# A two-layer decoder trunk: output and down projections with the tokens stationary and 512 weight columns moving

## The chip, the cores and the metric

The kernel runs on one core of one Trainium2 chip. The metric is the device time of one execution in microseconds (us); lower is better. The engines are named as the profile names them: PE is the tensor engine (PEld its weight loads), DVE the vector engine, ACT the scalar engine, POOL the general-purpose engine, and SP the engine whose queue issues the transfers.

## The reference

256 tokens of 2048 columns pass through two layers, all in float32. Cut to what matters here:

```python
for l in range(DEPTH):                                  # 2 layers
    h = rms_norm(x, norm_mix[l])                        # over 2048 columns
    proj = h @ w_in[l]                                  # 5446 columns, split among three kinds of heads
    o_a = diff_attention(dq, dk, dv, ...)               # 4 heads: (softmax(q1 k1) - lam softmax(q2 k2)) v, normed
    o_b = forgetting_attention(fq, fk, fv, ff, ...)     # 6 heads: logits + c[t] - c[s]
    o_c = latent_attention(mq, mkv, ...)                # 6 heads from low-rank q and kv
    x = x + concat(o_a, o_b, o_c) @ w_out[l]            # 2048 x 2048
    h = rms_norm(x, norm_ffn[l])
    x = x + square(relu(h @ w_ff_up[l])) @ w_ff_down[l] # 2048 x 8192 and 8192 x 2048
```

All attention is causal, over blocks of 128 queries, with normed queries and keys.

## The kernel before

**Arithmetic.** Weights and activations are multiplied as two float32r parts, hi and lo, that add up to the float32 value. `load_w` (L186) loads a raw weight tile of 128 x 1024 (five buffers), ACT copies it to `whi` (L193), DVE subtracts that to get `wlo` (L194), with three buffers of each. A product is hi x hi, lo x hi and hi x lo.

**Two forms of product.** `product_t` (L254) holds the weights stationary, 128 x 128 at a time. The moving operand is a chunk of the activations: both parts of 256 tokens, 512 columns, for `whi`, and the hi part alone, 256 columns, for `wlo`. So a weight tile of 1024 columns is 8 matmuls of 512 and 8 of 256, and the result has the weights' columns in the partitions and both parts of the tokens beside each other in one bank of PSUM. `product` (L269) holds 128 tokens stationary and lets the weights move, 512 columns wide in mq, dq, dk and dv: a tile of 1024 columns is two chunks by 512, and 12 matmuls of 512 columns. The input projection has the second form; the output projection (`wo`, L740 to 760), the up projection (`up_block`) and the down projection (`down_block`) have the first.

**The residual** `x` lies transposed: 16 chunks of 128 model columns in the partitions, by 256 tokens. `add_to_x` (L265) adds both halves of a bank to it, each 128 x 256, on DVE. `Norm.add` (L231) takes a finished chunk, multiplies it by the gain and splits it (`ht`), and squares it, summing the squares of all chunks on POOL; `Norm.scale` (L244) then sums over the partitions with eight one-column matmuls (`ss`) on PE. Layer 0's input comes transposed from memory (`FirstInput`, L364). The output is written transposed.

**Order.** A layer runs mq, mkv, the up projections of the latent heads, then fq, fk and fv in two halves, dq, dk, dv, the output projection, eight blocks of the feed-forward. Behind the products stand the steps of the attention heads, as generators in `Background` (`bg`, L80): after each weight tile `bg.step()` writes out 1.25 stages on the average, and `bg.finish()` all that are left. A scheduler then sorts the instructions of each engine by when it expects them to be ready, so that on PE a transpose or a score often stands in the middle of a tile's matmuls. The names that matter below are: `dt`, the transposes of the latent down projections `qd` and `kvd`; `qk`, transposes of queries and keys (`fqk`, `dqk`) or of the differential heads' outputs (`osb`); `s`, the scores; `p`, the exponentials, from `exps` (L312); `pt`, the transposes of p; `o`, p times the values. In `diff_maps` (L676) a head has two scores, p2 is scaled and taken from p1, and the result is transposed.

**The feed-forward.** `up_block` (L796) makes 1024 columns of the inner layer in eight banks of 128 columns; `squared` (L781) scales, clips and squares them and splits them into `g`. `down_block` (L810) adds 1024 rows of the down projection to all 16 chunks of x, one weight tile and one bank per chunk. While one block goes down, the next has already gone up.

Of the kernel before, what the change touches and what calls it, by code (L numbers as in the profile page):

```python
# [11 lines left out]
F32 = mybir.dt.float32  # L12
# [4 lines left out]
ALU = mybir.AluOpType  # L17
# [20 lines left out]
# Columns of w_in by group, in the order in which the groups are computed.  # L38
# [25 lines left out]
# Parameters along the free dimension, the same in every partition.  # L64
# [11 lines left out]
N_EARLY = 8  # L76
# [48 lines left out]
def trunk_kernel(ctx: ExitStack, tc: tile.TileContext, ins: dict, out: bass.AP):  # L125
# [15 lines left out]

    def mm(out, lhsT, rhs, start, stop):
        nc.tensor.matmul(out, lhsT, rhs, start=start, stop=stop)  # L143
# [15 lines left out]
    # The tensor engine's clock rises only with work: products of zeros until the first data are there.  # L159
# [9 lines left out]
    x = cp.tile([P, NK, SEQ], F32, name="x")  # transposed: chunks of the model's columns by tokens  # L169
# [8 lines left out]
    # Halves of these stay zero: one head's 64 rows beside the other's in a full contraction.  # L178
# [22 lines left out]
    def split_to(dst, src, gain):  # L201
        """dst [P, 2 parts, n] <- src [P, n] * gain [P, 1]"""
# [21 lines left out]
    class Norm:  # L224
        """The next norm's input, chunk by chunk: times gain and split into h, and squared into sums."""

        def __init__(self, gain, name):
            self.gain, self.name, self.h = gain, name, []
            self.squares = ap.tile([P, 2 * SEQ], F32, tag="squares", name=f"squares_{name}", bufs=1)

        def add(self, k):  # L231
            if k % 2 == 0:
                self.h.append(parts_tile("ht", "ht"))
            split_to(self.h[k // 2][:, k % 2], x[:, k, :], self.gain[:, k:k + 1])
            if k % 2 == 1:
                pair = x[:, k - 1:k + 1, :].rearrange("p c t -> p (c t)")
                if k == 1:
                    nc.scalar.activation(self.squares, pair, AF.Square)
                else:
                    sq = ap.tile([P, 512], F32, tag="sq", name="sq")  # L240
                    nc.scalar.activation(sq, pair, AF.Square)
                    nc.gpsimd.tensor_tensor(self.squares, self.squares, sq, ALU.add)

        def scale(self):  # L244
            """[P, NT] reciprocal root mean square of the tokens"""
# [66 lines left out]
    def exps(s):  # L312
        """exp(s - max) and the reciprocals of its sums; p holds the negated masked scores in between."""
# [15 lines left out]
    def transposed_p(p):  # L329
        """[keys, queries]: keys 0:128 by queries 0:256, then keys 128:256 by queries 128:256."""  # L330
# [7 lines left out]
    def weighted_values(pT, v, dst):  # L338
        """dst [P, 2 parts, tokens] <- (p @ v) transposed"""
# [5 lines left out]
    def heads_transposed(pairs):  # L345
        """Two [tokens, 128] blocks in both halves of the tokens, transposed into one bank."""
# [6 lines left out]
    def rotate(v, cos, sin, n, h):  # L353
        """v [P, n, 2, h] in place, by angles [P, h]"""
# [9 lines left out]
    class FirstInput:  # L364
        def __init__(self, norm):
            self.norm, self.n = norm, 0

        def __len__(self):
            return NK // 2

        def __getitem__(self, j):
            if j == self.n:
                self.n += 1
                nc.sync.dma_start(x[:, 2 * j:2 * j + 2, :], ins["xT"][:, 2 * j:2 * j + 2, :])
                self.norm.add(2 * j)
                self.norm.add(2 * j + 1)
                if j == 4:
                    nc.sync.dma_start(cst, ins["cst"])
            return self.norm.h[j]

    norm = Norm(pp[0][:, PP["mix"]], "mix0")
    h = FirstInput(norm)

    for l in range(DEPTH):
# [57 lines left out]
        # sums: [q rope, k rope | q nope, k nope] by tokens  # L442
# [35 lines left out]
        # small parameters of the layer  # L478
# [85 lines left out]
        def forget_gates():  # L564
# [8 lines left out]
            # log sigmoid(z) = min(z, 0) - log(1 + exp(-|z|)), log(1 + e) = 2 atanh(e / (2 + e))  # L573
# [14 lines left out]
            # Their running sums c, in rows by head (and -c six rows on), as three bfloat16 parts that add up  # L588
            # to them, 32 rows apart; with ones beside them a product over the rows gives c[t] - c[s].
# [146 lines left out]
        # some columns without the last heads, while those are worked on  # L736
# [195 lines left out]
```

## Time and profile before

| | us |
|---|---|
| median of three runs | 2173.51 |
| the three runs | 2173.34 to 2173.85 |
| span of the profiled execution | 2171.8 |
| PE busy | 2161.0 (100%), 12288 matmuls |
| DVE busy | 1494.2 (69%) |
| ACT busy | 1080.5 (50%) |
| POOL busy | 41.9 (2%) |

The profile shows one execution from its first to its last instruction; 1.7 us of the median lie outside that span. The granted clock of PE is full in every slice. Matmuls are pipelined: the shown duration of one reaches into the next, so the cost of a matmul in a row of them is read from start to start. The chain that ended last is followed back from the last instruction, at each step to what released it. In a row of the timeline, "x8" says how many instructions of one kind stand together, the second number is the time from the first one's start to the last one's end, and square brackets hold the idle time before it and what ended it.

### The profile page before, as it was taken

The numbers are of one execution on the slowest core, as the hardware profiler recorded it, in microseconds if no ns is written. First come the engines' busy times: TensorE is split into PE (matmuls) and PEld (weight loads), VectorE is DVE, ScalarE is ACT, GpSimd is POOL, SyncE is SP. The second block draws the span as 40 slices with busy tenths as digits, with TensorE's granted clock in tenths as the row PEclk, the third lists the DMA queues.
The fourth block names the chain that finished last, engine by engine and source line by source line (L and its number), as shares of the span: only waits on it lengthen the run. The fifth ranks groups of instructions, "written<-read, shape, count | busy, mean of one in ns | idle before, by whom it ended". The sixth has DMA issues, their size and how long they took to land.

```text
span 2171.8 us, 32348 instructions
## 1 busy us (share of the span) xinstructions
PE 2161.0 (100%) x12288; PEld 1917.7 (88%) x12288; DVE 1494.2 (69%) x2632; ACT 1080.5 (50%) x1587; POOL 41.9 (2%) x37
## 2 busy tenths in 40 slices
PE   9999999999999999999999999999999999999999
PEld 7999888888888888888899998888888888888888
DVE  7876687666666666666868667975666666566666
ACT  6655465544444444544566555645444444435442
POOL 2000001000000000000100000010000000000000
PEclk9999999999999999999999999999999999999999
DMA  7545455565556555555555464465556555555555
GB/s 237 172 140 179 155 160 190 182 192 186 189 187 191 188 187 191 186 191 186 189 161 170 139 182 151 151 204 186 192 185 192 186 190 189 188 191 186 192 184 155
DMA packets 116940, 393.81 MB, mean 181 GB/s; under 512 B 13232, under 2 KB 15408, under 8 KB 116784
## 3 DMA queue, kind: packets, MB, share of 16 engines
q1 hardware_dynamic: 116784, 391.74, 57.1%
q8 instruction: 97, 1.59, 0.3%
q14 instruction: 59, 0.48, 0.1%
HBM read 389.59 MB, written 2.10 MB: 180 GB/s over the span
## 4 chain that ended last, share of the span: by engine, by line
PE 94%; DVE 3%; ACT 1%; issue 1%; DMA 0%; SPq 0%; DVEq 0%
PE u L143 33%; PE dn L143 33%; PE wo L143 8%; PE fq L143 3%; PE fk L143 3%; PE fv L143 2%; PE dk L143 2%; PE dq L143 2%; PE mq L143 2%; PE s L143 2%; PE mkv L143 1%; PE qup L143 1%; DVE wlo L194 1%; PE o L143 1%; PE qk L299 1%
## 5 line engine op out<-in xcount | busy, mean ns | idle before, releaser
L193 ACT ACTIVATE whi<-wraw 128x1024 fp32r<-128x1024 f32 (+3 forms) x781 | 789.8, 1013 | 994.8 <-PE dn L143 389.7
L194 DVE TENSOR_TENSOR wlo<-wraw,whi 128x1024 fp32r<-128x1024 f32 (+3 forms) x781 | 910.2, 1166 | 410.2 <-ACT whi L193 401.2
L143 PE MATMUL u<-ht,whi 128*128 128x512 f32 x2048 | 513.1, 392 | 0.0
L143 PE MATMUL dn<-g,whi 128*128 128x512 f32 x2048 | 512.8, 392 | 0.0
L143 PEld LDWEIGHTS dn<-g,whi 128*128 128x128 f32 x2048 | 368.4, 189 | 65.8
L143 PEld LDWEIGHTS u<-ht,whi 128*128 128x128 f32 x2048 | 368.2, 189 | 65.9
L267 DVE TENSOR_TENSOR x<-dn,x 128x256 f32<-128x256 f32 x512 | 215.4, 422 | 205.9 <-PE dn L143 205.6
L143 PEld LDWEIGHTS u<-ht,wlo 128*128 128x128 f32 x2048 | 279.4, 190 | 20.0
L143 PEld LDWEIGHTS dn<-g,wlo 128*128 128x128 f32 x2048 | 279.4, 190 | 19.9
L143 PE MATMUL dn<-g,wlo 128*128 128x256 f32 x2048 | 285.6, 282 | 0.0
L143 PE MATMUL u<-ht,wlo 128*128 128x256 f32 x2048 | 285.6, 282 | 0.0
L143 PE MATMUL wo<-mix,whi 128*128 128x512 f32 x512 | 136.6, 400 | 0.0
L143 PEld LDWEIGHTS wo<-mix,whi 128*128 128x128 f32 x512 | 91.4, 189 | 15.3
L143 PEld LDWEIGHTS wo<-mix,wlo 128*128 128x128 f32 x512 | 72.0, 190 | 6.8 <-DVE wlo L194 0.6
L143 PE MATMUL wo<-mix,wlo 128*128 128x256 f32 x512 | 75.1, 283 | 0.0
L319 ACT ACTIVATE p<-p,nm 128x128 f32<-128x128 f32 x80 | 35.8, 449 | 40.3 <-DVE nm L318 40.2
L208 DVE SCALAR_TENSOR_TENSOR ht<-x,pp,ht 128x256 fp32r<-128x256 f32 x64 | 53.2, 847 | 3.0 <-ACT ht L207 2.8
L143 PE MATMUL fq<-whi,ht 128*128 128x384 f32 x256 | 53.7, 349 | 0.0
L787 DVE TENSOR_TENSOR relu<-u,relu 128x256 f32<-128x256 f32 x128 | 53.6, 419 | 0.0
L143 PE MATMUL fk<-whi,ht 128*128 128x384 f32 x256 | 51.7, 343 | 0.0
L143 PE MATMUL fv<-whi,ht 128*128 128x384 f32 x256 | 51.0, 340 | 0.0
L786 ACT COPY relu<-u 128x256 f32<-128x256 f32 x128 | 46.0, 359 | 0.0
(249 smaller groups left out, 1716.4 us busy)
## 6 DMA issues: line engine op xcount, KB each, us to landing
wraw<-in_w_up SPq DMA_DIRECT2D x256, 512.0 KB, 3.4
wraw<-in_w_down SPq DMA_DIRECT2D x256, 512.0 KB, 3.4
wraw<-in_w_out_c SPq DMA_DIRECT2D x32, 512.0 KB, 4.3
wraw<-in_w_fv SPq DMA_DIRECT2D x32, 384.0 KB, 3.2
wraw<-in_w_fq SPq DMA_DIRECT2D x32, 384.0 KB, 3.3
wraw<-in_w_fk SPq DMA_DIRECT2D x32, 384.0 KB, 3.1
wraw<-in_w_out_a SPq DMA_DIRECT2D x32, 384.0 KB, 3.1
wraw<-in_w_dq SPq DMA_DIRECT2D x16, 512.0 KB, 4.5
```

The lines of the kernel that those rows point to most:

```text
L143: nc.tensor.matmul(out, lhsT, rhs, start=start, stop=stop)
L193: nc.scalar.activation(hi[:, cols], raw[:, cols], AF.Copy)
L194: nc.vector.tensor_tensor(lo[:, cols], raw[:, cols], hi[:, cols], ALU.subtract)
L208: nc.vector.scalar_tensor_tensor(dst[:, 1, :], src, gain, dst[:, 0, :], ALU.mult, ALU.subtract)
L267: nc.vector.tensor_tensor(x[:, k, :], acc[:, i * SEQ:(i + 1) * SEQ], x[:, k, :], ALU.add)
L299: nc.tensor.transpose(dst, src, ident)
L319: nc.scalar.activation(p[:, cols], p[:, cols], AF.Exp, bias=nm[:, i:i + 1], scale=-1.0, accum_out=z[:, i:i + 1])
L786: nc.scalar.copy(r[:, cols], u[i][:, SEQ:])
L787: nc.vector.tensor_tensor(r[:, cols], u[i][:, :SEQ], r[:, cols], ALU.add)
```

## The change

Every matmul and transpose is now passed to `keep_in_program_order`: PE issues them in the order in which they are written, and the scheduler moves only the other engines' instructions.

The residual lies by tokens, two tiles of 128 tokens by 2048 columns. Output and down projections take the second form: `product_x` holds 128 tokens stationary, and each block of them meets two pieces of 512 weight columns in turn (one piece in the last 1024 columns of the output projection and of each layer's last down block). A tile is 12 matmuls of 512 columns. `add_to_x` adds a bank of 512 columns. The down projection is cut into two halves of 1024 columns, four banks each, with eight weight tiles after another into the same banks; up and down blocks take turns with the two pools of PSUM. The output projection does its first 1024 columns with the first 12 heads while the differential heads are worked on, then finishes the steps that are left, then adds the last four heads.

`Norm.columns` gets the transposed input of the next product from x: four transposes of 128 x 128 on PE into one bank (`xt`), whose halves are multiplied by the gain and split as before. The squares are summed along the rows by ACT as it squares; `Norm.scale` needs no matmul. Layer 0's first norm still reads the transposed input from memory (`FirstNorm`, with POOL and `ss` as before) into x's place, and x itself is loaded by four transfers of 512 KB during fq and fk of layer 0. The first up block works on four banks at once, first all over the first half of the columns. The output is written by tokens.

```diff
+    def in_order(ins):
+        tc.keep_in_program_order(ins)
+
     def mm(out, lhsT, rhs, start, stop):
-        nc.tensor.matmul(out, lhsT, rhs, start=start, stop=stop)
+        in_order(nc.tensor.matmul(out, lhsT, rhs, start=start, stop=stop))
...
-    x = cp.tile([P, NK, SEQ], F32, name="x")
+    x = cp.tile([P, NT, D_MODEL], F32, name="x")
...
+        def columns(self, c0, n):
+            for q in range(c0 // 512, (c0 + n) // 512):
+                for t in range(NT):
+                    junk = sp.tile([P, 512], F32, tag="junk", name="junk")
+                    nc.scalar.activation(junk, x[:, t, q * 512:(q + 1) * 512], AF.Square, accum_out=self.sums[:, t, q:q + 1])
+            for k in range(c0 // P, (c0 + n) // P, 2):
+                b = acc_tile("xt")
+                for i in range(2):
+                    for t in range(NT):
+                        transpose_block(b[:, i * SEQ + t * P:i * SEQ + (t + 1) * P], x[:, t, (k + i) * P:(k + i + 1) * P])
+                h = parts_tile("ht", "ht")
+                for i in range(2):
+                    split_to(h[:, i], b[:, i * SEQ:(i + 1) * SEQ], self.gain[:, k + i:k + i + 1])
+                self.h.append(h)
+                yield
...
-    def add_to_x(acc, k):
-        for i in (1, 0):
-            nc.vector.tensor_tensor(x[:, k, :], acc[:, i * SEQ:(i + 1) * SEQ], x[:, k, :], ALU.add)
+    def product_x(accs, chunk, hi, lo, off, start, stop):
+        c, j = chunk
+        for part, w in ((0, hi), (1, hi), (0, lo)):
+            for t in range(NT):
+                for b, acc in enumerate(accs[t]):
+                    mm(acc, c[:, j, part, t * P:(t + 1) * P], w[:, off + b * 512:off + (b + 1) * 512],
+                       start and w is hi and part == 0, stop and w is lo)
+
+    def add_to_x(accs, c0):
+        for t in range(NT):
+            for b, acc in enumerate(accs[t]):
+                cols = x[:, t, c0 + b * 512:c0 + (b + 1) * 512]
+                nc.vector.tensor_tensor(cols, acc, cols, ALU.add)
...
     def transpose_block(dst, src):
-        nc.tensor.transpose(dst, src, ident)
+        in_order(nc.tensor.transpose(dst, src, ident))
...
+                if l == 0:
+                    cols = slice((2 * s + a) * 512, (2 * s + a + 1) * 512)
+                    nc.sync.dma_start(x[:, :, cols], ins["x"][:, :, cols])
...
+        out_columns(left, w_left, 0, HALF, 0, N_EARLY, bg.step)
         bg.finish()
...
+        out_columns(left, w_left, 0, HALF, N_EARLY, 16)
+        add_to_x(left, 0)
+        bg.add(norm.columns(0, HALF))
+        for q in range(2):
+            c0 = HALF + q * 512
+            right = [[t_tile("wo")] for _ in range(NT)]
+            out_columns(right, lambda i: ins["w_out_b"][l, q, i], c0, 512, 0, 16, bg.step)
+            add_to_x(right, c0)
+            bg.add(norm.columns(c0, 512))
...
+            def block(bank, w, c0, width):
+                n, per = width // 512, 1024 // width
+                accs = [[bank("dn") for _ in range(n)] for _ in range(NT)]
+                for i in range(0, N_FC, per):
+                    hi, lo = load_w(w(i // per), 1024)
+                    for k in range(per):
+                        product_x(accs, chunks[i + k], hi, lo, k * width, i + k == 0, i + k == N_FC - 1)
+                    bg.step()
+                add_to_x(accs, c0)
```

Three places where PE's row differs. The first is in dq of layer 0, where the transposes of the forgetting heads' queries and keys (`fqk`) come in. Before:

```order
L143 MATMUL dq_2268<-whi,ht 128x512 x2
L143 MATMUL dq_2269<-whi,ht 128x512 x2
L143 MATMUL dq_2268<-whi,ht 128x512 x2
L143 MATMUL dq_2269<-whi,ht 128x512 x2
L299 MATMUL qk<-cst,fqk_1860 128x128
L143 MATMUL dq_2268<-wlo,ht 128x512
L299 MATMUL qk<-cst,fqk_1861 128x128
L299 MATMUL qk<-cst,fqk_1860 128x128
L299 MATMUL qk<-cst,fqk_1861 128x128
L143 MATMUL dq_2268<-wlo,ht 128x512
L143 MATMUL dq_2269<-wlo,ht 128x512 x2
```

The same place in PE's row after the change:

```order
L148 MATMUL dq_2272<-wlo,ht 128x512 x2
L148 MATMUL dq_2273<-wlo,ht 128x512 x2
L359 MATMUL qk<-cst,fqk_1862 128x128
L359 MATMUL qk<-cst,fqk_1863 128x128
L359 MATMUL qk<-cst,fqk_1862 128x128
L359 MATMUL qk<-cst,fqk_1863 128x128
L148 MATMUL dq_2272<-whi,ht 128x512 x2
L148 MATMUL dq_2273<-whi,ht 128x512 x2
L148 MATMUL dq_2272<-whi,ht 128x512 x2
L148 MATMUL dq_2273<-whi,ht 128x512 x2
```

The eight matmuls by `whi` of the next tile, which stood ahead of these transposes, now stand behind them.

The second place is in dv of layer 0, at the transposes of the differential heads' queries and keys (`dqk`; the two numbers are the two halves of the tokens). Before:

```order
L143 MATMUL dv_2719<-wlo,ht 128x512 x2
L299 MATMUL qk<-cst,dqk_2265 128x128 x2
L143 MATMUL dv_2718<-whi,ht 128x512 x2
L143 MATMUL dv_2719<-whi,ht 128x512 x2
L143 MATMUL dv_2718<-whi,ht 128x512 x2
L143 MATMUL dv_2719<-whi,ht 128x512
L299 MATMUL qk<-cst,dqk_2266 128x128
L299 MATMUL qk<-cst,dqk_2265 128x128
L299 MATMUL qk<-cst,dqk_2266 128x128 x2
L299 MATMUL qk<-cst,dqk_2265 128x128
L299 MATMUL qk<-cst,dqk_2266 128x128
L143 MATMUL dv_2719<-whi,ht 128x512
```

After:

```order
L148 MATMUL dv_2723<-wlo,ht 128x512 x2
L359 MATMUL qk<-cst,dqk_2269 128x128
L359 MATMUL qk<-cst,dqk_2270 128x128
L359 MATMUL qk<-cst,dqk_2269 128x128
L359 MATMUL qk<-cst,dqk_2270 128x128
L359 MATMUL qk<-cst,dqk_2269 128x128
L359 MATMUL qk<-cst,dqk_2270 128x128
L359 MATMUL qk<-cst,dqk_2269 128x128
L359 MATMUL qk<-cst,dqk_2270 128x128
L148 MATMUL dv_2722<-whi,ht 128x512 x2
```

The seven matmuls of the next tile that stood between the first half's transposes and the second half's now follow all eight.

The third place is in the output projection of layer 0, at the second score of a differential head (`half_106`) and the transposes of p. Before:

```order
L143 MATMUL s<-kT,half_106 128x128
L143 MATMUL s<-kT,half_106 128x256
L143 MATMUL wo<-mix_0_841,whi 128x512 x2
L143 MATMUL wo<-mix_1_842,whi 128x512
L299 MATMUL pt<-cst,p 128x128
L143 MATMUL wo<-mix_1_842,whi 128x512
L143 MATMUL wo<-mix_2_843,whi 128x512
L299 MATMUL pt<-cst,p 128x128 x2
L143 MATMUL wo<-mix_2_843,whi 128x512
L143 MATMUL wo<-mix_0_841,wlo 128x256 x2
L143 MATMUL wo<-mix_1_842,wlo 128x256 x2
L143 MATMUL wo<-mix_2_843,wlo 128x256 x2
```

After:

```order
L148 MATMUL s<-kT,half_102 128x128
L148 MATMUL s<-kT,half_102 128x256
L148 MATMUL wo<-whi,mix_0_841 128x512 x8
L148 MATMUL wo<-wlo,mix_0_841 128x512 x4
L148 MATMUL s<-kT,half_106 128x128
L148 MATMUL s<-kT,half_106 128x256
L359 MATMUL pt<-cst,p 128x128 x6
L359 MATMUL qk<-cst,dqk_2269 128x128
L359 MATMUL qk<-cst,dqk_2270 128x128
```

Before, the three transposes shown are those of the head whose scores came earlier, and those of this head's p follow another nine to eleven products later; now the transposes of both heads follow at once on the score.

## Rows read from the trace of the kernel before

**Rows 1.** The page: busy engines (us, share, instructions), the transfer queue, the last chain.
```profile
PE 2161.0 (100%) x12288; PEld 1917.7 (88%) x12288; DVE 1494.2 (69%) x2632; ACT 1080.5 (50%) x1587; POOL 41.9 (2%) x37
...
q1 hardware_dynamic: 116784, 391.74, 57.1%
...
PE 94%; DVE 3%; ACT 1%; issue 1%; DMA 0%; SPq 0%; DVEq 0%
```

**Rows 2.** The chain of waits (start us, us, what), one down block.
```profile
464.82 44.69 PE dn L143 x256
```

**Rows 3.** The timeline (start us, us, engine, line, operation), PE, an up tile.
```profile
906.00 2.00 PE L143 MATMUL u<-ht,whi 128*128 128x512 f32 x8
907.84 1.11 PE L143 MATMUL u<-ht,wlo 128*128 128x256 f32 x8
```

**Rows 4.** The timeline, PE, a tile of mq in layer 1 and the next.
```profile
1098.55 1.98 PE L143 MATMUL mq<-whi,ht 128*128 128x512 f32 x8
1100.36 1.07 PE L143 MATMUL mq<-wlo,ht 128*128 128x512 f32 x4
1101.27 1.98 PE L143 MATMUL mq<-whi,ht 128*128 128x512 f32 x8
```

**Rows 5.** The page's costliest groups (count, busy us, mean ns, idle), dn and wo.
```profile
L143 PE MATMUL dn<-g,whi 128*128 128x512 f32 x2048 | 512.8, 392 | 0.0
...
L143 PE MATMUL wo<-mix,whi 128*128 128x512 f32 x512 | 136.6, 400 | 0.0
```

**Rows 6.** Timeline, PE, transposes in mkv of layer 1; the group pt (ns min/median/max).
```profile
1118.23 0.87 PE L299 MATMUL dt<-cst,qd 128*128 128x128 f32 x6
1118.86 0.85 PE L143 MATMUL mkv<-wlo,ht 128*128 128x326 f32 x4
...
L299 PE MATMUL pt<-cst,p x96: 270/272/328, 98.3 to 1376.5; 128*128 128x128 f32 x96
```

**Rows 7.** The timeline, PE, the sums of squares in layer 0's feed-forward.
```profile
379.43 1.05 PE L143 MATMUL ss<-cst,squares_ffn 128*128 128x1 f32 x8
380.34 2.09 PE L143 MATMUL u<-ht,whi 128*128 128x512 f32 x8
```

**Rows 8.** Groups by line (ns min/median/max), DVE, adds of 256 and scalings of 512 columns.
```profile
L267 DVE TENSOR_TENSOR x<-dn,x x512: 407/421/426, 467.7 to 2168.5; 128x256 f32<-128x256 f32 x171
...
L788 DVE SCALAR_TENSOR_TENSOR relu<-relu,rsb x64: 691/693/695, 388.0 to 2080.4; 128x512 f32<-128x512 f32 x64
```

**Rows 9.** The timeline, PE, scores to transposed p of differential heads in both layers.
```profile
278.42 0.82 PE L143 MATMUL s<-kT,half 128*128 128x128 f32 x4
...
278.88 1.05 PE L143 MATMUL wo<-mix,whi 128*128 128x512 f32 x3
...
284.06 0.38 PE L299 MATMUL pt<-cst,p 128*128 128x128 f32 x2
...
1356.23 0.82 PE L143 MATMUL s<-kT,half 128*128 128x128 f32 x4
...
1362.12 0.27 PE L299 MATMUL pt<-cst,p 128*128 128x128 f32 x1
```

**Rows 10.** The timeline, PE, transposes of fqk in dq of layer 0.
```profile
202.71 1.97 PE L143 MATMUL dq<-whi,ht 128*128 128x512 f32 x8
...
205.00 0.30 PE L299 MATMUL qk<-cst,fqk 128*128 128x128 f32 x1 [0.33 <-DVE fqk L619]
```

**Rows 11.** The timeline, PE, transposes of dqk in dv of layer 0.
```profile
265.25 0.38 PE L299 MATMUL qk<-cst,dqk 128*128 128x128 f32 x2
265.39 1.87 PE L143 MATMUL dv<-whi,ht 128*128 128x512 f32 x7
...
267.62 0.88 PE L299 MATMUL qk<-cst,dqk 128*128 128x128 f32 x6 [0.36 <-DVE dqk L361]
```

**Rows 12.** The timeline, PE and ACT, transposes of qd in mkv of layer 0.
```profile
37.02 1.21 PE L143 MATMUL mkv<-whi,ht 128*128 128x326 f32 x7
...
37.72 1.25 ACT L395 ACTIVATE qd<-mq,y_mix 128x512 f32<-128x512 f32 x2
...
38.44 0.33 PE L299 MATMUL dt<-cst,qd 128*128 128x128 f32 x1 [0.22 <-ACT qd L395]
```

More of the change, by code (lines that the diff above doesn't have):

```diff
@@ L75 @@
 N_FC = FB // P
-N_EARLY = 8
+HALF = D_MODEL // 2
+N_EARLY = 12
 WARM = 12
@@ L222, in rsqrt_of, with h, __len__, __getitem__ @@
         return y
-    class Norm:
+    class FirstNorm:
         def __init__(self, gain, name):
-            self.gain, self.name, self.h = gain, name, []
+            self.gain, self.name, self.parts = gain, name, []
             self.squares = ap.tile([P, 2 * SEQ], F32, tag="squares", name=f"squares_{name}", bufs=1)
[L231 to L237, printed above, removed]
+        @property
+        def h(self):
+            return self
+        def __len__(self):
+            return NK // 2
+        def __getitem__(self, j):
+            if j == len(self.parts):
+                pair = x.rearrange("p n d -> p (n d)").rearrange("p (c t) -> p c t", t=SEQ)[:, 2 * j:2 * j + 2, :]
+                nc.sync.dma_start(pair, ins["xT"][:, 2 * j:2 * j + 2, :])
+                self.parts.append(parts_tile("ht", "ht"))
+                for i in range(2):
+                    split_to(self.parts[j][:, i], pair[:, i, :], self.gain[:, 2 * j + i:2 * j + i + 1])
+                pair = pair.rearrange("p c t -> p (c t)")
+                if j == 0:
                     nc.scalar.activation(self.squares, pair, AF.Square)
@@ L251, in scale, with __init__ @@
             nc.vector.tensor_copy(ss, b[:, :NT])
+            return rsqrt_of(ss, NT, [(slice(0, NT), D_MODEL)], self.name)
+    class Norm:
+        def __init__(self, gain, name):
+            self.gain, self.name, self.h = gain, name, []
+            self.sums = sp.tile([P, NT, D_MODEL // 512], F32, tag="sums", name=f"sums_{name}")
+        def columns(self, c0, n):
[9 more added lines that the diff above has]
+                h = parts_tile("ht", "ht")
+                for i in range(2):
+                    split_to(h[:, i], b[:, i * SEQ:(i + 1) * SEQ], self.gain[:, k + i:k + i + 1])
+                self.h.append(h)
+                yield
+        def scale(self):
+            ss = sp.tile([P, NT], F32, tag="ssm", name=f"ss_{self.name}")
+            nc.vector.tensor_reduce(ss, self.sums, AX.X, ALU.add)
             return rsqrt_of(ss, NT, [(slice(0, NT), D_MODEL)], self.name)
@@ L777, in trunk_kernel @@
         bg.add(scale_rows())
-        h_chunks = [(h[k // 2], k % 2) for k in range(NK)]
         def squared(u, g):
@@ L794, in squared, with up_block, down_block @@
             yield
-        def up_block(fb):
+        def up_block(fb, bank):
             tiles = []
-            for j in range(N_FC // 2):
-                u = [t_tile("u") for _ in range(2)]
-                first = fb == 0 and j == 0
-                for i, half_k in ((0, 0), (1, 0), (0, 1), (1, 1)) if first else ((0, 0), (0, 1), (1, 0), (1, 1)):
-                    w = load_w(ins["w_up"][l, fb * N_FC + 2 * j + i, half_k], 1024)
-                    product_t(u[i], h_chunks[half_k * 8:half_k * 8 + 8], *w, 0, half_k == 0, half_k == 1)
-                    bg.step()
-                tiles.append(parts_tile("mt", "g"))
-                bg.add(squared(u, tiles[-1]))
-            return tiles
-        def down_block(fb, tiles):
+            per = 4 if fb == 0 else 1
+            for j in range(0, N_FC, per):
+                u = [bank("u") for _ in range(per)]
+                for half_k in range(2):
+                    for i in range(per):
+                        while len(h) < 4 * (half_k + 1):
+                            bg.one()
+                        w = load_w(ins["w_up"][l, fb * N_FC + j + i, half_k], 1024)
+                        chunks = [(h[k // 2], k % 2) for k in range(half_k * 8, half_k * 8 + 8)]
+                        product_t(u[i], chunks, *w, 0, half_k == 0, half_k == 1)
+                        bg.step()
+                for i in range(per):
+                    waiting.append(u[i])
+                    if len(waiting) == 2:
+                        tiles.append(parts_tile("mt", "g"))
+                        bg.add(squared(tuple(waiting), tiles[-1]))
+                        waiting.clear()
+            return tiles
+        waiting = []
+        def down_block(fb, tiles, first, second):
             nonlocal norm, h
             last = fb == N_FB - 1
+            bg.finish()
             if last and l + 1 < DEPTH:
@@ L815, in down_block @@
                 h = norm.h
-            bg.finish()
             chunks = [(tiles[k // 2], k % 2) for k in range(N_FC)]
-            for j in range(NK):
-                acc = acc_tile("dn")
-                product_t(acc, chunks, *load_w(ins["w_down"][l, fb, j], 1024), 0, True, True)
-                add_to_x(acc, j)
+            def block(bank, w, c0, width):
+                n, per = width // 512, 1024 // width
+                accs = [[bank("dn") for _ in range(n)] for _ in range(NT)]
+                for i in range(0, N_FC, per):
+                    hi, lo = load_w(w(i // per), 1024)
+                    for k in range(per):
+                        product_x(accs, chunks[i + k], hi, lo, k * width, i + k == 0, i + k == N_FC - 1)
+                    bg.step()
+                add_to_x(accs, c0)
                 if last and l + 1 < DEPTH:
-                    norm.add(j)
+                    bg.add(norm.columns(c0, width))
                 elif last:
-                    nc.sync.dma_start(out[j * P:(j + 1) * P, :], x[:, j, :])
-        g = up_block(0)
+                    for t in range(NT):
+                        nc.sync.dma_start(out[t * P:(t + 1) * P, c0:c0 + width], x[:, t, c0:c0 + width])
+            block(first, lambda i: ins["w_down_a"][l, fb, i], 0, HALF)
+            if last:
+                for q in range(2):
+                    block(second, lambda i: ins["w_down_c"][l, q, i], HALF + q * 512, 512)
+            else:
+                block(second, lambda i: ins["w_down_b"][l, fb, i], HALF, HALF)
+        banks = [t_tile, acc_tile]
+        g = up_block(0, banks[0])
         for fb in range(N_FB):
-            g_next = up_block(fb + 1) if fb + 1 < N_FB else None
-            down_block(fb, g)
+            g_next = up_block(fb + 1, banks[(fb + 1) % 2]) if fb + 1 < N_FB else None
+            down_block(fb, g, banks[fb % 2], banks[(fb + 1) % 2])
             g = g_next
```

68 lines of the change are left out of this document (22 added, 46 removed).

## The prediction

> **What bounds the kernel now.** I read the page's busy line first: the tensor engine (PE) is busy all through the span, and the chain that ended last is PE for 94% of it [rows 1]. So the end moves by what PE has to issue, plus the times at which PE stands still for another engine. Next the chain of waits: one block of the down projection, 16 weight tiles, is one unbroken piece of 44.69 us [rows 2], which is 2.793 us per tile with nothing in it but PE. The vector engine (DVE) and the scalar engine (ACT) have slack there, as the page shows (69% and 50%) [rows 1]; that PE is what ends last holds in all the stages that the change touches.
>
> PE's work is priced by start-to-start times, since the duration of one matmul overlaps the next. The timeline of a block of this form gives 8 matmuls of 512 columns in 906.00 to 907.84, 230 ns each [rows 3]; the 8 of 256 columns take the rest of 2.793, 119 ns each. The same arithmetic with the tokens stationary is in the kernel already: the product mq takes 12 matmuls of 512 columns from 1098.55 to 1101.27, so 2.720 us per tile [rows 4], 226.7 ns each.
>
> **The change part by part.**
>
> Down and output projection. The matmuls of 512 columns by hi-parts of the weights in dn and wo are 2048 and 512, eight to a tile [rows 5], so 256 and 64 tiles, 320 in all. Columns moved per tile stay 6144 (8 x 512 + 8 x 256 before, 12 x 512 after); four matmuls less per tile save their fixed part. By mq's price each tile gains 2.793 - 2.720 = 0.073 us, so **-23.4 us**, all of it on PE's path. The bounds: if the new form cost dn's own 230 ns for 512 columns, a tile would be 2.760 and the gain 10.6; if the second of two matmuls in a row with the same stationary block (six pairs a tile, 1920 in all) had no fixed part, the gain would be larger; that part is 8 ns or so, since 256 columns more cost 230 - 119 = 111 ns and 256 columns alone 119, so 15.4 us more. I take mq's price, because its operands stand as the new ones do; no row shows a pair that shares a block.
>
> [...]
>
> Transposes. Three norms now take their columns from x by tokens: 3 x 32 = 96 blocks of 128 x 128 on PE, in 24 banks. Six dt transposes fill 1118.23 to 1118.86 [rows 6], 105 ns each, and the matmul behind a group is a little late itself; I take 110: **+10.6 us**. Their adds, squares and copies go to ACT and DVE with a weight tile (2.72 us) between an x add and the first transpose: the new add is 512 wide, 0.69 us as the row of the same width in the feed-forward shows [rows 8], and the first transposes wait for three of the four adds. These are 2.1 us that begin 0.7 us before the block's last tile ends, so they are done 1.4 us into the next tile's 2.7: covered. Without that cover it would be 1.4 us at each of nine places. The first feed-forward block goes by four tiles over the first half of the columns, then four over the second, so the last columns have 11 us: 0.
>
> [...]
>
> Sums of squares. Three of the four norms lose their eight one-column matmuls, 379.43 to 380.34, with a slower restart [rows 7]: about 1.0 us each, **-3.0 us**. The 512 adds of 256 columns of dn at 0.42 [rows 8] become 128 of 512 columns at 0.69, off DVE and not off PE; nothing waits there, so this is 0. The extra reload of x (four transfers of 512 KB on SP's queue in layer 0) meets transfer engines that are busy for 57% of the span [rows 1]: 0, at worst 1.
>
> The kept order. Every matmul and transpose now runs in the order written, and this is where I expect the gain to go. Before, PE's attention steps were spread between products, and what wasn't ready stood behind products that were. Now PE waits, and each product behind it with it:
> - Layer 0, dt. PE is through with two mkv tiles at 37.02; the copies of qd run from 37.72 to 38.97; before, 7 products were done in between and the wait was 0.22 [rows 12]. 1.95 less that and a transpose: +1.6.
> - Layer 0, dq. The qk transposes of fqk come right after a tile that ends at 202.71; DVE has scaled fqk at 205.00, and a wait of 0.33 was paid before [rows 10]: +1.9.
> - dv in both layers. The eight qk of dqk now stand together at 265.25, but half of them need the rotation that is ready at 267.6; before, 7 products lay in between [rows 11]. 2.3 less the transposes that can go and the 0.36: +1.7, and the same in layer 1: 3.5 in all.
> - Softmax. From the scores of half_106 (278.42, the next product starts at 278.88) to the transposes of its p at 284.06 it is 5.2 us, mostly ACT's exponents and DVE's scaling [rows 9]; before, nearly two tiles of products lay between. In layer 0's first pair nothing lies between now but the other head's transposes: 5.2, less 0.8 of DVE's x adds that are gone, less 0.7 of work and waits that were there, +3.7. In the second pair one tile of 2.7 lies between, but two scores stand together, so the second is late by the first's turn on DVE: +3.0. In layer 1 one tile lies between with a chain from 1356.23 to 1362.12 [rows 9]: +0.8 at each of two places.
> - Small ones: three steps of the forgetting heads in layer 0, one an earlier transpose (0.3), two where the copy of pt is waited for at once (0.6, 0.7), the last heads' product right behind their own transposes in both layers (2 x 0.6), a bank of dv that the output projection takes over (0.8), and two wide adds at the end of the program (0.5): +4.1, estimates from copies of 0.4 to 0.5 us and DVE steps of 0.42 and 0.69.
> Together 1.6 + 1.9 + 3.5 + 3.7 + 3.0 + 1.6 + 4.1 = **+19.4 us**. Bounds: 8, if the chains shorten because DVE has no x adds and shorter queues, and 27, if each chain takes its full length.
>
> Sum: -23.4 + 10.6 - 3.0 + 19.4 = +3.6 on a span of 2171.8, so 2175.4. The median of the three times is 1.7 above that span; the time is **2177 us**.
>
> **Rivals.**
> *The waits are covered (A).* While PE waits, ACT and DVE go on with the splits of later tiles, and then the chain behind it is faster than before's trace shows. With 5 us of waits: 2162.7. For it: DVE is idle for 31% of the span. Against: each chain here is a row of dependent steps of 0.2 to 0.5 us, which no idle time shortens.
> *512 columns cost 230 ns (B), the slower side.* In dn and u the matmul of 512 columns takes 230 [rows 3], in mq 226.7 [rows 4]. If the width and not the form sets that in the long blocks, the gain is 10.6 and the time 2189.9. It decides from 226.9 ns on, where the loss passes 0.2%. [...]
> *Shared stationary blocks (C).* The second of each pair loses its 8 ns: 2177 - 15.4 = 2161.6. Nothing in the rows speaks for it but that the fixed part is there.
> *Transposes at their duration (D).* 96 x 0.272 = 26.1 instead of 10.6: 2192.6. The dt group at 105 ns speaks against it.
>
> **How the numbers follow.** Chances: forecast 0.56 (own range 2168 to 2184), A 0.20, B 0.13, C 0.06, D 0.05. About 0.2%, some 4.3 us, is what a measurement of this kernel can tell from no change: 2169.2 to 2177.9 is the same. Of the forecast 0.04 lies below this, 0.36 within and 0.16 above, since it sits near the upper edge. Faster is 0.04 + 0.20 + 0.06 = 0.30, same 0.36, slower 0.16 + 0.13 + 0.05 = 0.34. The range leaves out C, D and the far end of A: 2162 to 2190.
>
> **What would show it.** In the profile after: a dn tile at 2.72 us in a steady block, some 44.69 - 1.2 = 43.5 us for 16 tiles; xt groups at 0.44 us; no ss but layer 0's first; and PE idle of some 20 us more in the groups dt, qk and pt, released by DVE and ACT. I am wrong if the steady blocks differ from 43.5 by more than 0.3 (B or C), or if the added idle of PE is below 8 or above 27 us.

## The result, and the profile after

| | before, us | after, us |
|---|---|---|
| median | 2173.68 (2173.34 to 2174.12, 4 runs) | 2187.56 (2185.74 to 2188.22, 4 runs) |
| span of the profiled execution | 2171.8 | 2185.7 |
| PE busy | 2161.0 | 2158.2, with 1208 matmuls fewer |
| DVE busy | 1494.2 | 1359.8 |

The changed kernel is slower: the ratio is 1.0062, with a 95% interval of 1.0048 to 1.0076. By the prediction's own lines that is slower, to which it gave 0.34, and not the same, to which it gave 0.36. The time is 10.6 us above the predicted 2177. It lies inside the range of 2162 to 2190, but 3.6 us above the forecast's own band of 2168 to 2184.

The page of the changed kernel, its line of busy engines (the answer to [rows 1]):

```profile
PE 2158.2 (99%) x11080; PEld 1864.3 (85%) x11080; DVE 1359.8 (62%) x2160; ACT 1085.4 (50%) x1603; POOL 12.7 (1%) x16
```

PE still works nearly from end to end. It issues less and ends later, so the time lies between its instructions and in their spacing. Of the span PE stands still for 27.5 us, where it was 10.8 before: 16.7 more. The chain of waits is read in the kernel without the kept order (first experiment below), where it reaches further back, for blocks of the same instructions (the answer to [rows 2]):

```profile
1760.35 44.67 PE u L148 x256
1805.01 43.55 PE dn L148 x192
1848.56 44.67 PE u L148 x256
```

A down block falls from 44.69 to 43.55 us. In the changed kernel a tile of such a block reads, on PE's timeline:

```profile
571.42 2.00 PE L148 MATMUL dn<-whi,g 128*128 128x512 f32 x8
573.26 1.07 PE L148 MATMUL dn<-wlo,g 128*128 128x512 f32 x4
574.17 0.62 PE L148 MATMUL dn<-whi,g 128*128 128x512 f32 x2
```

From 571.42 to 574.17 it is 2.75 us for this one, and 43.55 / 16 = 2.72 on the average.

Where did the time go? The table takes, for each stage, the time from the start of its first product matmul to the start of the next stage's. Stages that differ by less than 0.3 us in every column are left out; the third column is the first experiment.

| stage | before | after | after, order not kept |
|---|---|---|---|
| mq, mkv, layer 0 | 27.11 + 15.89 | 27.53 + 17.35 | 27.81 + 15.84 |
| first fv and fq, layer 0 | 42.59 | 43.23 | 42.57 |
| second fq, layer 0 | 22.53 | 23.31 | 22.55 |
| dq, layer 0 | 27.47 | 29.49 | 27.45 |
| dk, layer 0 | 24.23 | 24.99 | 24.23 |
| dv, layer 0 | 24.45 | 27.74 | 24.45 |
| wo, layer 0 | 100.42 | 109.87 | 102.37 |
| six down blocks, each layer | 6 x 44.69 | 6 x 43.55 | 6 x 43.55 |
| last two down blocks, layer 0 | 89.39 | 91.43 | 90.33 |
| mkv, layer 1 | 15.58 | 15.28 | 15.28 |
| dv, layer 1 | 24.32 | 27.75 | 24.32 |
| wo, layer 1 | 100.07 | 103.92 | 102.33 |
| last two down blocks and the end | 93.34 | 93.64 | 92.54 |

Twelve down blocks give back 13.7 us. The attention stages and the output projection take 26. The first row also holds the wait for the first loads: mq of layer 0 takes 26.9 to 27.8 us in the nine kernels of this document, with the order kept and without.

PE's timeline of the changed kernel at six of the places, with what ended each idle time (the first four are the answers to [rows 12], [rows 10], [rows 11] and [rows 9]; the last two are the second such wait in layer 0's output projection and the one in dv of layer 1):

```profile
36.70 0.76 PE L148 MATMUL mkv<-wlo,ht 128*128 128x326 f32 x4
38.73 0.33 PE L359 MATMUL dt<-cst,qd 128*128 128x128 f32 x1 [1.26 <-ACT qd L437]
...
204.96 1.07 PE L148 MATMUL dq<-wlo,ht 128*128 128x512 f32 x4
208.15 0.89 PE L359 MATMUL qk<-cst,fqk 128*128 128x128 f32 x4 [2.12 <-DVE fqk L661]
...
271.20 0.27 PE L359 MATMUL qk<-cst,dqk 128*128 128x128 f32 x1
273.56 0.98 PE L359 MATMUL qk<-cst,dqk 128*128 128x128 f32 x7 [2.10 <-DVE dqk L421]
274.30 3.31 PE L148 MATMUL dv<-whi,ht 128*128 128x512 f32 x8
277.41 1.47 PE L148 MATMUL dv<-wlo,ht 128*128 128x512 f32 x4
...
290.18 0.83 PE L359 MATMUL pt<-cst,p 128*128 128x128 f32 x3
293.49 0.83 PE L359 MATMUL pt<-cst,p 128*128 128x128 f32 x3 [2.48 <-DVE p L735]
...
314.39 0.83 PE L359 MATMUL pt<-cst,p 128*128 128x128 f32 x3 [1.75 <-DVE p L735]
...
1359.11 0.55 PE L359 MATMUL qk<-cst,dqk 128*128 128x128 f32 x3 [2.10 <-DVE dqk L421]
```

The idle times in brackets are the waits of the prediction. The row at 274.30 is something else: eight matmuls of 512 columns need 3.11 us to the next start, where the tile shown above needs 1.84. The view of stretches (length; busy time of PE, PEld, DVE, ACT, POOL; granted clock; DMA share, GB/s) tells what happened there:

```profile
275.00:278.50 3.50, 3.50 (x11) 2.70 (x10) 1.67 (x6) 0.85 (x1) 0.00 (x0) 0.54 0.80 288
294.00:298.00 4.00, 4.00 (x23) 3.43 (x24) 1.07 (x3) 1.89 (x4) 0.00 (x0) 1.00 0.21 85
316.00:319.00 3.00, 3.00 (x8) 2.32 (x8) 0.58 (x2) 1.05 (x5) 0.00 (x0) 0.50 0.06 23
1361.00:1363.00 2.00, 2.00 (x6) 1.63 (x5) 0.00 (x0) 0.51 (x1) 0.00 (x0) 0.50 0.85 258
```

In three stretches (first, third and fourth row; the first row's window ends a little later than its stretch) the granted clock is half (0.54, 0.50 and 0.50 in the rows, where full is 1.00), and a matmul of 512 columns takes 427 ns from start to start instead of 227. Each follows a wait of PE, of 2.10, 1.75 and 2.10 us. Behind the longest wait of all, the 2.48 us at 293.49, the clock stayed full (1.00, second row). A fourth stretch of half clock lies at the start, from 8.6 us on (0.50 over 8.60 to 11.00), where PE waits for its first loads; in the kernel before PE waits there too and the clock is full (1.00 over the same time), and the stage mq is only 0.4 us shorter.

### The profile page after: what moved, and what is told of

It is laid out like the page before. It is cut to its first block, busy times and chain, and to the rows that moved or that the text cites. A ratio compares the mean times of both kernels' runs of the same rounds, so it can differ in the third digit from the quotient of the medians.

```text
span 2185.7 us, 29225 instructions
## 1 busy us (share of the span) xinstructions
PE 2158.2 (99%) x11080; PEld 1864.3 (85%) x11080; DVE 1359.8 (62%) x2160; ACT 1085.4 (50%) x1603; POOL 12.7 (1%) x16
## 5 line engine op out<-in xcount | busy, mean ns | idle before, releaser
L148 PE MATMUL dn<-whi,g 128*128 128x512 f32 x2048 | 511.2, 390 | 0.9 <-ACT whi L198 0.4
L148 PEld LDWEIGHTS dn<-whi,g 128*128 128x128 f32 x2048 | 383.0, 188 | 82.0 <-DVE x L327 2.3
L148 PE MATMUL dn<-wlo,g 128*128 128x512 f32 x1024 | 276.3, 389 | 0.0
L148 PEld LDWEIGHTS dn<-wlo,g 128*128 128x128 f32 x1024 | 192.2, 188 | 40.0
L148 PE MATMUL wo<-whi,mix 128*128 128x512 f32 x512 | 138.8, 403 | 0.3
L148 PEld LDWEIGHTS wo<-whi,mix 128*128 128x128 f32 x512 | 95.3, 190 | 20.1 <-ACT mix L212 0.7
L327 DVE TENSOR_TENSOR x<-dn,x 128x512 f32<-128x512 f32 x128 | 79.7, 684 | 26.1 <-PE dn L148 26.1
L148 PE MATMUL wo<-wlo,mix 128*128 128x512 f32 x256 | 73.9, 390 | 0.0
L148 PEld LDWEIGHTS wo<-wlo,mix 128*128 128x128 f32 x256 | 48.3, 188 | 10.6
L832 DVE SCALAR_TENSOR_TENSOR relu<-relu,rsb 128x512 f32<-128x512 f32 x64 | 44.3, 692 | 2.3
```

Of the source, the lines that this page charges most:

```text
L148: in_order(nc.tensor.matmul(out, lhsT, rhs, start=start, stop=stop))
L327: nc.vector.tensor_tensor(cols, acc, cols, ALU.add)
L832: nc.vector.scalar_tensor_tensor(r, r, 0.0, rsb2, ALU.max, ALU.mult)
```

## The experiments

**Theory:** the kept order makes PE wait, and half clock behind some of the waits adds to it; the products' gain is real. **Rival:** the waits come with the new layout, its banks and copies, and the order is harmless.

### The changed kernel without the kept order

```diff
     def in_order(ins):
-        tc.keep_in_program_order(ins)
+        pass
```

> The changed kernel without the kept order: matmuls and transposes may be moved by the scheduler again, all else as changed. Theory (the kept order makes PE stand still, some 20 us of waits and 4.7 us of half clock behind three of them; the new products' gain of 23 us is real): 2187.6 falls to 2162 to 2168, the stall before the qk of dqk in dv shrinks from 2.3 to under 0.6 us in both layers and the one of 2.6 us before pt in the output projection too, and the granted clock is full throughout. Rival (the waits come from the new layout, banks and copies, and the order is harmless): 2184 to 2190 with the waits at the same places.

Measured: 2163.89 us (2163.69 to 2163.95, 5 runs), a ratio to before of 0.9954 with an interval of 0.9940 to 0.9967, and a granted clock of 0.999 to 1.000 in the five. That is 23.7 us less than the changed kernel and 10 less than the kernel before. PE's timeline in dv and in the output projection:

```profile
265.69 0.38 PE L359 MATMUL qk<-cst,dqk 128*128 128x128 f32 x2
265.82 1.87 PE L148 MATMUL dv<-whi,ht 128*128 128x512 f32 x7
268.05 0.88 PE L359 MATMUL qk<-cst,dqk 128*128 128x128 f32 x6 [0.35 <-DVE dqk L421]
...
281.61 0.43 PE L359 MATMUL pt<-cst,p 128*128 128x128 f32 x2
281.80 1.86 PE L148 MATMUL wo<-whi,mix 128*128 128x512 f32 x7
283.50 1.07 PE L148 MATMUL wo<-wlo,mix 128*128 128x512 f32 x4
284.41 0.39 PE L148 MATMUL wo<-whi,mix 128*128 128x512 f32 x1
284.64 0.27 PE L359 MATMUL pt<-cst,p 128*128 128x128 f32 x1
```

The seven products stand between the two halves' transposes again, as in [rows 11], and a tile of products between the two heads' pt. The rival falls: at these places the new layout without the order has the waits of the kernel before (0.35 us here, 0.36 in [rows 11]). From 30 to 2150 us of the span PE stands still for 2.5 us in the kernel before, 19.0 in the changed kernel and 4.3 in this one.

### The kernel before with the kept order alone

```diff
-        nc.tensor.matmul(out, lhsT, rhs, start=start, stop=stop)
+        tc.keep_in_program_order(nc.tensor.matmul(out, lhsT, rhs, start=start, stop=stop))
...
-        nc.tensor.transpose(dst, src, ident)
+        tc.keep_in_program_order(nc.tensor.transpose(dst, src, ident))
```

> The kernel before with the kept order alone: residual, products and norms as before. Theory (the order costs what it cost in the changed kernel): 2173.7 rises by 17 to 26 us, to 2191 to 2200, with PE waiting at dt, at qk of fqk and dqk and at pt of the differential heads, and stretches of half clock behind some of these. Rival (the order is harmless by itself, the waits need the new layout): 2173 to 2178.

Measured: 2205.66 us (2204.93 to 2206.95, 4 runs), 31.7 us more than before, ratio 1.0147 (1.0133 to 1.0161). The order alone costs more than the 17 to 26 us that I expected. The stages show where: the two output projections are 11.6 and 6.7 us longer than before, where the order costs 7.5 and 1.6 in the changed kernel. A likely reason, which was not tested, is that in the old program the steps are written closer together there: a step stands behind each 768-column tile, which is three quarters of a full one. One of the waits on PE's timeline, ahead of the transposes of the last heads' outputs in layer 0, where PE stands still for 0.14 and 0.27 us in the changed kernel:

```profile
327.19 0.33 PE L299 MATMUL qk<-cst,osb 128*128 128x128 f32 x1 [1.34 <-DVE osb L719]
327.79 0.77 PE L299 MATMUL qk<-cst,osb 128*128 128x128 f32 x3 [0.27 <-DVE osb L719]
328.21 2.91 PE L143 MATMUL wo<-mix,whi 128*128 128x512 f32 x6
```

Behind them six matmuls take 2.71 us, at half clock again. With the order kept on both sides, the rest of the change is worth 2205.66 - 2187.56 = 18.1 us; with the order free on both sides, 10.1.

### PE kept busy during four of the waits

```diff
+    def fill(bank, n):
+        for _ in range(n):
+            mm(bank, zeros[:, :P], zeros, True, True)
...
-    def transposed_p(p):
+    def transposed_p(p, n=0):
         pt = t_tile("pt")
+        fill(pt, n)
...
-            dpT[i] = transposed_p(p1)
+            dpT[i] = transposed_p(p1, (0, 10, 0, 8)[i] if l == 0 else 0)
```

The transposes of `dqk` of the first head get ten such products in the same way. They are products of zeros into the bank that the transposes then fill.

> The changed kernel with products of zeros put ahead of three long waits of PE, into the bank that is written next: 10 ahead of the first qk of dqk in dv of each layer, 10 and 8 ahead of two pt in layer 0's output projection (8 to 10 times 0.21 us, no longer than the wait). The waits for DVE stay, PE is only busy in them. Theory (each such wait is followed by 7 or 8 matmuls at 427 instead of 227 ns because PE stood still): the half-clock stretches at dv of both layers and in layer 0's output projection go, 4.7 us less: 2182 to 2184. Rival (the clock falls for another reason, or the loss is the wait alone): 2187 to 2190, stretches still there.

Measured: 2184.01 us (2182.68 to 2184.39, 5 runs), 3.5 us less with 38 matmuls more. PE's timeline at dv of layer 0:

```profile
272.94 2.33 PE L148 MATMUL qk<-zeros 128*128 128x512 bf16 x10
275.10 1.17 PE L359 MATMUL qk<-cst,dqk 128*128 128x128 f32 x8
276.03 2.08 PE L148 MATMUL dv<-whi,ht 128*128 128x512 f32 x8
277.95 1.07 PE L148 MATMUL dv<-wlo,ht 128*128 128x512 f32 x4
```

Four stretches of that kernel, behind dv, the first pt, the second pt, and then dq (columns as above):

```profile
276.00:279.00 3.00, 3.00 (x17) 2.51 (x16) 2.28 (x8) 1.47 (x3) 0.00 (x0) 1.00 0.89 285
294.00:298.00 4.00, 3.93 (x24) 3.34 (x23) 0.89 (x4) 1.87 (x3) 0.00 (x0) 1.00 0.29 108
315.00:319.00 4.00, 3.99 (x23) 3.49 (x24) 0.58 (x2) 2.06 (x6) 0.00 (x0) 1.00 0.37 127
209.00:213.00 4.00, 4.00 (x13) 3.13 (x12) 1.73 (x8) 1.30 (x2) 0.00 (x0) 0.58 0.37 125
```

The ten products of zeros take 2.16 us to the next start, 216 ns each. Behind the filled waits the clock is full (1.00) and the eight matmuls take 1.92 us. The stages are shorter by 1.63 (dv, layer 0), 1.48 (wo, layer 0) and 1.60 us (dv, layer 1), together the 4.7 that I expected. But in this execution the clock is half behind the wait at dq (last row, 0.58 over 209 to 213), which was not filled and behind which it had been full in the changed kernel's profile; that costs 1.62, and so 3.1 is left, as the two profiled spans differ (2185.7 and 2182.6), and near the 3.5 of the medians. Behind the four filled waits there is no half clock (behind the first pt there was none in the changed kernel's profile either). That fits the theory that it belongs to the standing still, in one execution. Which of the other waits it follows differs from run to run.

### The two pools of banks swapped in the last down block

```diff
+            if last:
+                first, second = second, first
             block(first, lambda i: ins["w_down_a"][l, fb, i], 0, HALF)
...
-                b = acc_tile("xt")
+                b = self.bank("xt")
```

The next layer's `xt` move to the other pool too, so that none waits for a bank of a running product.

> The changed kernel with the two pools of PSUM banks swapped in each layer's last down block (first half into the pool that the block before last did not just use, the next layer's xt into that pool as well). Theory (the last block's first four matmuls each wait 0.3 to 0.4 us for a bank that the x adds of the half before still read, 1.4 us a layer): 2.8 us less, 2184.5 to 2185.5, and the four waits ahead of the last block gone in both layers. Rival (the wait only moves, to the xt banks or the next piece): 2187 to 2189.

Measured: 2182.45 us (2182.14 to 2185.37, 5 runs), 5.1 us less, where I expected 2.8. The stages of the last two down blocks are 89.88 and 92.08 instead of 91.43 and 93.64, so 3.1 of it is the banks. The rest is of the size by which the half clock can differ from run to run, which is not shown for it: the profile of this kernel is of the slowest of its five runs, 2185.37, and has four stretches of half clock behind the first loads, where the changed kernel's has three. DVE, PE and its weight loads in the changed kernel at that place:

```profile
1055.55 2.48 DVE L327 TENSOR_TENSOR x<-dn,x 128x512 f32<-128x512 f32 x4 [0.63 <-PE dn L148]
1056.39 2.91 PE L148 MATMUL dn<-whi,g 128*128 128x512 f32 x7 [0.20 <-ACT whi L198]
1056.89 0.19 PEld L148 LDWEIGHTS dn<-whi,g 128*128 128x128 f32 x1 [0.35 <-DVE x L327]
1057.49 0.19 PEld L148 LDWEIGHTS dn<-whi,g 128*128 128x128 f32 x1 [0.41 <-DVE x L327]
```

Seven matmuls take 2.91 us to the end of the last one; at 227 ns a start that would be 1.75. The first four go into four banks that the four adds, from 1055.55 on, free one after another; the weight loads show the waits for them (0.35 and 0.41 us, released by DVE's adds). The same place with the pools swapped:

```profile
1055.69 1.07 PE L148 MATMUL dn<-wlo,g 128*128 128x512 f32 x4
1056.59 1.07 PE L148 MATMUL dn<-whi,g 128*128 128x512 f32 x4
```

### Each xt transpose twice

```diff
                     for t in range(NT):
-                        transpose_block(b[:, i * SEQ + t * P:i * SEQ + (t + 1) * P], x[:, t, (k + i) * P:(k + i + 1) * P])
+                        for _ in range(2):
+                            transpose_block(b[:, i * SEQ + t * P:i * SEQ + (t + 1) * P], x[:, t, (k + i) * P:(k + i + 1) * P])
```

> The changed kernel with each xt transpose issued twice, 96 more. Theory (a transpose costs PE its start-to-start time, 109 to 111 ns): 10 to 11 us more, 2197.5 to 2199. Rival (it costs its duration of 272 ns): 26 us more, 2213. Second rival (the transposes lie in time that PE has left over): under 3 us more.

Measured: 2197.75 us (2195.85 to 2199.43, 4 runs), 10.2 us more for 96 transposes, 106 ns each. The group's row in that kernel (ns min/median/max):

```profile
L360 PE MATMUL xt<-cst,x x192: 270/272/273, 348.6 to 1488.2; 128*128 128x128 f32 x192
```

This prices further transposes in a row. What the 96 themselves cost is read in the changed kernel, at a group in the output projection:

```profile
348.88 0.60 PE L359 MATMUL xt<-cst,x 128*128 128x128 f32 x4
349.23 1.17 PE L148 MATMUL wo<-whi,mix 128*128 128x512 f32 x4
350.24 0.62 PE L148 MATMUL wo<-wlo,mix 128*128 128x512 f32 x2
```

Four transposes take 0.35 us to the next start, and the four products behind them 1.01 us instead of 0.91, so a group costs 0.45, where the prediction looked for 0.44. All 96 start to start are 8.7 us, and with 0.1 behind each of their 22 uninterrupted rows it is 10.8 or so. The duration of 272 ns is not the price.

### No shared stationary block in two matmuls in a row

```diff
-            for t in range(NT):
-                for b, acc in enumerate(accs[t]):
+            for b in range(len(accs[0])):
+                for t in range(NT):
+                    acc = accs[t][b]
```

> The changed kernel with the two inner loops of the product exchanged: the token halves alternate within a 512-column piece, so that no two matmuls in a row share a stationary block. Theory (each matmul pays its full spacing whether or not its neighbour has the same block): a down block stays at 43.5 us, 2187 to 2188.5. Rival (shared blocks save, or cost, part of the weight load): the block moves by over 0.3 us and the whole by over 5 us.

Measured: 2186.24 us (2185.22 to 2186.82, 4 runs), and each of the twelve down blocks at 43.55 us to the hundredth, as in the changed kernel. A tile of one on PE's timeline takes 2.75 us from start to start, as the changed kernel's at 571.42 does:

```profile
572.52 2.00 PE L148 MATMUL dn<-whi,g 128*128 128x512 f32 x8
574.36 1.07 PE L148 MATMUL dn<-wlo,g 128*128 128x512 f32 x4
575.27 0.62 PE L148 MATMUL dn<-whi,g 128*128 128x512 f32 x2
```

A matmul here pays its spacing of 227 ns whether its neighbour has the same block or not.

### Both edits: order free, pools swapped

> The changed kernel without the kept order and with the pools swapped in the last down block: both edits at once. If the two are independent, the time is that of the kernel without the order less 2.8 us, 2159 to 2165, below the kernel before (2173.7). If the scheduler already hides the wait for the banks by moving other work ahead, it equals the kernel without the order within 1 us.

Measured: 2162.80 us (2161.27 to 2163.91, 5 runs), ratio to before 0.9948 (0.9934 to 0.9961). It is 1.1 us below the kernel without the order, whose runs it overlaps. In its profile the last two down blocks are 0.45 us shorter in each layer (89.88 and 92.09), 0.9 together, and the rest of the span takes the same time: where products may move, they cover most of the wait for the banks. Its median is the lowest of the study, and like the kernel with the order free it beats both the kernel before and the changed one.

## Why the prediction was right or wrong

**The products.** Right. The forecast took mq's 2.720 us a tile and 43.5 a block; it is 43.55 in every steady block. Rival B, a block bound by 230 ns, is out, and so is C, shared blocks, which was tried. On the output projection the wo matmuls fall from 92.07 to 90.34 us in layer 0 and from 92.02 to 90.70 in layer 1, start to start without PE's idle time, with the order free. All in all -1.14 x 16 - 1.7 - 1.3 = -21.2 where -23.4 was forecast. About 1 us of the difference is the late start of the wo matmuls behind groups of `xt`, which the price of the transposes holds as well.

**The transposes.** Right: +10.2 measured for 96 further ones, and some 10.8 for the 96 themselves, against +10.6. The x adds were covered as forecast, as far as the transposes go: PE stands still ahead of none of them. Rival D, a price of 272 ns each as the row of pt shows it for the duration [rows 6], is out.

**The sums of squares.** The first up block gains 0.13 us with two groups of `xt` in the place of one `ss`. Doubling the two groups costs 0.83 more, so `ss` cost about 1.0, as forecast. It is left in layer 0's first norm only.

**The kept order.** The step was right and is most of the result: taking the order away gives 23.7 us. PE's idle time grew by 16.7 us, inside the 8 to 27 that the prediction set as its sign. Its terms can be compared one by one with the stages, changed kernel less the kernel without the order:

| place | forecast | measured | of it half clock |
|---|---|---|---|
| dt, layer 0 | 1.6 | 1.5 | |
| three steps of the forgetting heads | 1.6 | 2.2 | |
| qk of fqk, dq | 1.9 | 2.0 | |
| qk of dqk, dv, layer 0 | 1.7 | 3.3 | 1.6 |
| qk of dqk, dv, layer 1 | 1.7 | 3.4 | 1.6 |
| softmax, wo, layer 0 | 6.7 | 7.5 | 1.5 |
| softmax, wo, layer 1 | 1.6 | 1.6 | |
| last down blocks, two | none | 2.2 | |

Without half clock the waits of the named places are 16.8 against 16.8 forecast. That the sums agree so closely is luck, since single places are off by up to 0.7, and the row of layer 0's output projection also holds the bank of dv (0.8 forecast; the first eight products there take 2.40 us, 2.08 with the order free). Rival A, that ACT and DVE would be faster behind a waiting PE, is out. The chain ahead of the qk of dqk is 2.36 us with the order kept and free, and 2.37 before. The one from a score to its pt in layer 1 is 4.4 us with the order kept and free; it is shorter than the 5.9 before, so it is the new layout that shortened it and not PE's waiting.

**What failed** is two things that the sum has no term for. The first is the clock: I costed a wait at its own length, and three waits of about 2 us were followed by 1.5 to 1.6 us each of lost time at half clock, 4.7 in all. The trace of before doesn't show it: behind the first loads PE waits there for at most 0.4 us at a time, and the granted clock is 1.000. The second is a bank: the sentence that found the x adds covered looked at the transposes behind them, and not at the products. The last down block follows the one before without an up block in between, so it meets the pool of banks that the adds have just begun to read, 3.1 us over both layers. The second could have been read from the order of the changed program.

**Small terms.** The transposes of `osb` take 1.71 us a layer, start to start, with the order free and kept alike, from 0.74 and 0.82 before: they stand ahead of the last heads' products, and the free order puts nothing between. The forecast had put 0.6 a layer to the order. The end of the program costs 2.28 - (93.34 - 92.09) = 1.0 us more than before with the pools swapped, where 0.5 was forecast.

The parts with the order free: -21.2 + 10.2 - 3.0 + 1.9 (osb) + 1.0 (end) = -11.1, against 2163.89 - 2173.98 = -10.1 measured; what the banks still cost there is 1.1 (both edits), which closes the sum to 0.1, though terms of up to 0.7 us, such as mq of layer 0, are not in it and are taken to cancel. The order and what it brings with it: +23.7. So the median is 10.6 above the forecast: 4.7 of it is half clock, 3.1 the banks, 2.2 the products' gain that was sized too high, and 0.6 is left for the small terms.

The time lies above the forecast's band of 2168 to 2184, and it is inside the stated range only because that reached to 2190 for rival B, products at 230 ns, which is not what happened. To that extent the range held by luck. The chance of 0.56 for the forecast was too high and the one of 0.34 for slower too low. I had given the waits a range of 8 to 27 and put the outcome near its middle; with the half clock and the banks counted in, the order costs 23.7.

## What to carry to other kernels

When a change fixes the order of a busy engine, list each place at which the written order has a consumer right behind its producer's chain; the length of that chain in the old trace gave the cost here to within 0.7 us at each place, without the half clock that followed some of the waits. Look also at what a pool of banks meets when a loop's last turn leaves out the stage between two users. A gain in the arithmetic and a loss in the order are best separated: here the first was worth 10 us and the second 24, and the version that keeps only the first is one line away.

## What the runs showed of the hardware that was not expected

Stretches of half clock lie behind waits of PE in the middle of work, at a price of 1.4 to 1.6 us each. The six profiles with the kept order have 18 of them between the first loads and PE's last product. Each begins between 0.5 us before and 1.6 us after the end of a wait of 1.3 to 2.5 us, and none lies elsewhere; the profiles with the order free, whose waits there are under 0.9 us, have none. The length of the wait alone doesn't decide it. Of the six profiles, the wait of 2.1 us at dq was followed by half clock in five (0.50 to 0.69 over 209.50 to 212.50) and not in the changed kernel's (1.00); the wait of 2.1 us at dv of layer 0, filled in one, was followed by it in the changed kernel alone; and the wait of 2.5 us ahead of pt, which the changed kernel passed at full clock, was followed by it in the four others that did not fill it (0.50 to 0.63 over 294.50 to 297.50). Two rows of the stretch 209.50 to 212.50, of the changed kernel and of the one with the pools swapped, where the program up to there is the same:

```profile
209.50:212.50 3.00, 3.00 (x17) 2.49 (x16) 1.59 (x6) 1.36 (x3) 0.00 (x0) 1.00 0.36 142
```

```profile
209.50:212.50 3.00, 3.00 (x8) 2.24 (x8) 0.47 (x3) 1.06 (x1) 0.00 (x0) 0.50 0.11 45
```

What decides between the two was not tried. It is the likely reason that the changed kernel's runs spread over 2.5 us and those of the kernel before over 0.8. That is argued, not shown, though the mean granted clock of the runs points the same way: in the kernel with the filled waits it is 1.000 in the fastest run, 2182.68 us, and 0.998 in the slowest, 2184.39.
